# The first four hidden tiles of each down projection are loaded into the raw weight ring

## The chip, the cores and the metric

The kernel runs on one core of one Trainium2 chip. The metric is the device time of one execution in microseconds; a profiled execution has a span (first to last instruction) and a time of its own that is a little longer. Both are given below.

## The reference, cut to what matters

Two layers, each a mixer (stick-breaking attention with an S5 scan in the first, gated delta rule in the second) followed by a squared-ReLU MLP. The change lies in the MLP, which runs once in each layer:

```python
def sq_relu_mlp(h, w1, w2):            # h: 1040 x 1024, w1: 1024 x 4096, w2: 4096 x 1024
    return jnp.square(jax.nn.relu(h @ w1)) @ w2
...
    hn = rms_norm(hs, pre_mlp_norm[i])
    hs = hs + rms_norm(sq_relu_mlp(hn, mlp_w1[i], mlp_w2[i]), post_mlp_norm[i])
return hs[:, N_META:]
```

There are 1024 tokens and 16 meta tokens in front of them, so 1040 columns (NT); the model width is 1024 and the hidden width 4096. All of it is float32.

## The kernel before, in words

**Layout and precision.** Activations lie transposed: the feature is the partition, the token the column. Every float32 factor of a matmul is split into a high part (a cast to the matmul's float32r format) and a low part (the value minus the high part), and each product is three matmuls: high by high, low by high, high by low (`unit`, L176 to L178). For weights the two parts are `whi` and `wlo`, for the hidden activations of the down projection `hh` and `hl`.

**Buffers.** All large tiles come out of one ring of 33 slots of 128 by 1048 (`slot`, tag `r4`): the split activations, the accumulators `acc`, the hidden tiles. Beside them stand two raw tiles of 128 by 1040 (`raw`, tag `wraw`), into which every weight tile is loaded before it is split, and four `whi` and four `wlo` tiles. A matmul accumulates in one of eight PSUM banks: three named `mm`, three `tr`, two `ax`.

**The MLP (`mlp`), up phase.** The hidden activations are computed 128 rows at a time and written to DRAM (`hd`, 32 tiles): six tiles directly (`up`), the other 26 in 13 pairs (`pair`), each a Strassen-like product of seven half-size products (`product`, L478 to L480). `ops` loads the two weight tiles of a pair into the two raw tiles and forms seven operands from them. The result of a product goes through VectorE (L487, and L491 for the ReLU), ScalarE squares it (L415) and a DMA writes it out (L416); its temporaries are called p, u and c.

**The MLP, down phase.** `acc`, eight accumulators, then 14 groups of two hidden tiles and a last group of four (`down`). For group g the code asks for `hidden(2g)` and `hidden(2g+1)`, then for the two w2 tiles (`weight`, with `act=True`):

- `hidden(k)` loads row tile k of `hd` into a raw buffer named `hr` (L529, on SyncE's DMA queue), ScalarE casts it to `hh` (L228), GpSimd subtracts to `hl` (L229).
- `weight` loads a w2 tile into one of the two `wraw` tiles (L156, the same DMA queue), ScalarE casts `whi` (L163), GpSimd subtracts `wlo` (L166).
- `gemm` then walks eight output tiles m and, in each, the column chunks (three of 352, 344, 344 columns in the first layer; two of 512 in the second). One such (m, chunk) is a unit: six matmuls for the group's two k, then VectorE copies the PSUM bank to `acc` (L552, first group) or adds it to `acc` (L554, later groups). A group has 24 units in the first layer and 16 in the second. Six PSUM banks are used in turn (`six`).

Below, h0, h1, ... stand for the hidden tiles in this phase and w0, w1, ... for the w2 tiles; group 0 is h0, h1 with w0, w1, group 1 is h2, h3 with w2, w3.

**What sets the order.** The code's order is not the order on the engines. The framework schedules each engine's instructions when the program is built, and it hands out the buffers of a ring while it does so. What it settles is fixed: each engine, and SyncE's DMA queue too, then works its list strictly in order and stops at an instruction whose buffer or input is not there. One list on SyncE issues nearly all transfers of the kernel; the casts of hidden and weight tiles and the squares of the up phase share ScalarE's list, and the subtractions share GpSimd's.

Of the kernel before, what the change touches and what calls it, by code (L numbers as in the profile page):

```python
# [50 lines left out]
class Net:  # L51
# [349 lines left out]
    def mlp(self, layer, st, hs_d, chunks, gpre, ahead=None):  # L401
# [122 lines left out]

        def hidden(k):

            raw = self.slot("hr")
            hi, lo = self.slot("hh", F32R), self.slot("hl", F32R)
            nc.sync.dma_start(raw[:, t0:NT], hd[:, k, t0:NT])  # L529
            self.split(hi[:, t0:NT], lo[:, t0:NT], raw[:, t0:NT], lo_eng=nc.gpsimd)  # L530
            hid[k] = (hi, lo)

        def down(ks, last=False):
            first = ks[0] == 0
            for k in ks:
                hidden(k)
            W = {k: self.weight(w2[layer, k], act=True) for k in ks}
            out, hook, ch = None, None, wide
            if last:
                ch = chunks  # L540
                if ahead is None:
                    ch = CH3
                if ahead is not None:
                    ahead()
                ssq = self.slot("ssq_o")
                reuse = [t for k in ks for t in hid[k]]
                *out, hook = self.residual(acc, ssq, reuse, G_POSTMLP + 8 * layer, hs_d, gpre, ch)

            def ev(m, c, pt):
                o, n = ch[c]  # L550
                if first:
                    nc.vector.tensor_copy(acc[m][:, o:o + n], pt)  # L552
                else:
                    nc.vector.tensor_add(acc[m][:, o:o + n], pt, acc[m][:, o:o + n])  # L554
                if last:
                    self.sq_acc(ssq, m, m == 0, acc[m][:, o:o + n], o, n)

            self.gemm(range(8), ks, lambda m, k: tuple(w[:, m * 128:(m + 1) * 128] for w in W[k]), lambda k: hid[k], ch, "c" if last else "m", ev, hook, None if last else six)
            for k in ks:
                del hid[k]  # L560
            return out
# [1583 lines left out]
```

## Time and profile before

| | |
|---|---|
| Time, 3 executions | 2953.96, 2966.62, 2972.64 us; median 2966.62 |
| Profiled execution: its time | 2961.22 us |
| Profiled execution: its span | 2959.2 us |
| Mean granted TensorE clock | 0.942 |
| TensorE matmul busy | 2771.1 us, 94% of the span |
| TensorE weight load busy | 2506.0 us, 85% |
| VectorE, ScalarE, GpSimd busy | 1764.7, 1064.4, 1311.6 us |
| Transfers | 360.99 MB, mean 122 GB/s |

In the rows of the profile, a group of instructions reads: line, engine, operation, output tile <- input tiles, shapes, count, and behind a bar its busy time, the mean of one in ns, and the idle time of the engine just before, with what ended it. A row of the timeline reads: start in us, duration, engine, line, operation, tiles, count, and in brackets the idle time before it and its releaser. PE is TensorE, PEld its weight loads, DVE VectorE, ACT ScalarE, POOL GpSimd, SPq SyncE's DMA queue. A row that merges n instructions (xn) gives the start of the first and the time until the last has ended. In the row of a stretch, behind the busy times of the five engines, stand the granted clock, the DMA share and GB/s. The first layer's MLP passes from the up phase to the down phase at about 1047 to 1069 us of the span, the second layer's at about 2554 to 2575 us.

### The profile page before, as it was taken

To read this page: it belongs to the slowest core of one execution; us is meant where nothing else is said; L and a number is where in the kernel's file an instruction comes from. 1 tells how busy PE (TensorE), PEld (TensorE's weight loads), DVE (VectorE), ACT (ScalarE), POOL (GpSimd) and SP (SyncE) were. 2 spreads that over 40 slices of the span, in tenths; PEclk is the share of its full clock that TensorE was granted. 3 is DMA by queue.
4 is the path that set the end of the run, shared out by engine and by line. 5 is a ranking of instruction groups with operands and counts; after the bars stand their busy time and mean duration, and the time that the engine had idled before them with its cause. 6 is when DMAs were issued, how large, how long until landed. Compare 5 with 4: busy or idle time off the path is not lost. (4 is left out here: it accounts for less than half of the span.)

```text
span 2959.2 us, 44165 instructions
## 1 busy us (share of the span) xinstructions
PE 2771.1 (94%) x16488; PEld 2506.0 (85%) x16488; DVE 1764.7 (60%) x3107; ACT 1064.4 (36%) x2108; POOL 1311.6 (44%) x942
## 2 busy tenths in 40 slices
PE   7799998999999999999897978999998999999997
PEld 6689666888999999999887877889998888878887
DVE  8643778677665555555846995444537444544445
ACT  4111556554543332110436322444435433321201
POOL 5561325225577755342522132111135777655423
PEclk9899568899999999999998988999999999999999
DMA  3435212134433343221426667443424333333222
GB/s 128 155 129 161 78 46 88 47 100 167 133 114 102 105 150 130 87 85 57 132 92 216 204 207 208 144 131 126 141 90 158 111 114 107 128 142 100 94 83 87
DMA packets 209766, 360.99 MB, mean 122 GB/s; under 512 B 45488, under 2 KB 131200, under 8 KB 209552
## 3 DMA queue, kind: packets, MB, share of 16 engines
q1 hardware_dynamic: 205664, 353.49, 37.0%
q10 hardware_dynamic: 3888, 4.69, 0.4%
q8 instruction: 130, 2.13, 0.3%
q14 instruction: 84, 0.69, 0.1%
HBM read 247.07 MB, written 111.03 MB: 121 GB/s over the span
## 5 line engine op out<-in xcount | busy, mean ns | idle before, releaser
L166 POOL TENSOR_TENSOR wlo<-wraw,whi 128x1024 fp32r<-128x1024 f32 x129 | 316.4, 2466 | 786.0 <-ACT whi L163 303.4
L176 PE MATMUL mm<-ahi,whi 128*128 128x344 f32 (+2 forms) x1200 | 416.1, 347 | 43.0 <-DVE cx L1333 29.2
L178 PE MATMUL mm<-ahi,wlo 128*128 128x344 f32 (+2 forms) x1200 | 397.3, 331 | 2.3 <-DVE wlo L166 2.3
L177 PE MATMUL mm<-hl,whi 128*128 128x352 f32 (+4 forms) x1136 | 388.8, 342 | 7.2 <-POOL hl L229 7.2
L554 DVE TENSOR_TENSOR acc<-mm,acc 128x344 f32<-128x344 f32 (+4 forms) x308 | 177.3, 576 | 198.2 <-PE mm L178 198.2
L176 PEld LDWEIGHTS mm<-ahi,whi 128*128 128x128 f32 x1200 | 233.8, 195 | 51.2 <-DVE cx L1333 30.7
L176 PE MATMUL mm<-hh,whi 128*128 128x352 f32 (+4 forms) x752 | 260.0, 346 | 5.3 <-ACT hh L228 4.6
L178 PE MATMUL mm<-hh,wlo 128*128 128x352 f32 (+4 forms) x752 | 259.9, 346 | 5.0 <-POOL wlo L166 5.0
L178 PEld LDWEIGHTS mm<-ahi,wlo 128*128 128x128 f32 x1200 | 233.2, 194 | 4.4 <-DVE wlo L166 3.2
L177 PEld LDWEIGHTS mm<-hl,whi 128*128 128x128 f32 x1136 | 218.1, 192 | 19.6 <-POOL hl L229 8.4
L554 DVE TENSOR_TENSOR acc<-tr,acc 128x344 f32<-128x344 f32 (+2 forms) x260 | 152.9, 588 | 137.2 <-PE tr L178 137.2
L163 ACT CAST whi<-wraw 128x1024 fp32r<-128x1024 f32 x77 | 77.5, 1044 | 361.1 <-PE tr L177 357.9
L177 PE MATMUL tr<-hl,whi 128*128 128x512 f32 (+2 forms) x560 | 197.2, 352 | 0.0
L178 PE MATMUL tr<-hh,wlo 128*128 128x512 f32 (+2 forms) x560 | 197.1, 352 | 0.0
L176 PE MATMUL tr<-hh,whi 128*128 128x512 f32 (+2 forms) x560 | 196.9, 352 | 0.0
L229 POOL TENSOR_TENSOR hl<-hr,hh 128x1040 fp32r<-128x1040 f32 (+1 forms) x64 | 155.2, 2434 | 84.6 <-ACT hh L228 69.3
L178 PEld LDWEIGHTS mm<-hh,wlo 128*128 128x128 f32 x752 | 142.8, 190 | 16.6 <-POOL wlo L166 6.2
L176 PEld LDWEIGHTS mm<-hh,whi 128*128 128x128 f32 x752 | 142.7, 190 | 16.3 <-ACT hh L228 5.3
L440 POOL TENSOR_TENSOR wlo<-sS,whi 128x512 fp32r<-128x512 f32 x104 | 144.6, 1393 | 13.8 <-ACT whi L439 13.7
L228 ACT CAST hh<-hr 128x1040 fp32r<-128x1040 f32 (+1 forms) x64 | 67.4, 1054 | 172.3 <-DMA hr<-hd 164.2
L177 PE MATMUL mm<-hh,whi 128*128 128x344 f32 (+2 forms) x384 | 129.3, 337 | 0.0
L244 POOL TENSOR_TENSOR ssq<-ssq,sq 128x344 f32<-128x344 f32 (+2 forms) x84 | 91.4, 1088 | 84.6 <-ACT sq L243 76.6
(526 smaller groups left out, 7825.8 us busy)
## 6 DMA issues: line engine op xcount, KB each, us to landing
wraw<-w SPq DMA_DIRECT2D x128, 512.0 KB, 3.6
hr<-hd SPq DMA_DIRECT2D x32, 520.0 KB, 5.4
wraw<-wino SPq DMA_DIRECT2D x32, 512.0 KB, 5.0
hr<-hd SPq DMA_DIRECT2D x32, 512.0 KB, 4.4
dm<-dmd SPq DMA_DIRECT2D x16, 520.0 KB, 5.5
hsd<-hs SPq DMA_DIRECT2D x48, 172.0 KB, 1.9
hd<-u SPq DMA_DIRECT2D x52, 130.0 KB, 3.3
hd<-u SPq DMA_DIRECT2D x26, 256.0 KB, 2.2
```

Source lines behind the costliest of these rows:

```text
L163: nc.scalar.copy(hi[:, :n], raw[:, :n])
L166: (nc.vector if fast else nc.gpsimd).tensor_sub(lo[:, :n], raw[:, :n], f(hi[:, :n]))
L176: nc.tensor.matmul(pt, wh, h[:, o:o + n], start=i == 0, stop=False)
L177: nc.tensor.matmul(pt, wh, l[:, o:o + n], start=False, stop=False)
L178: nc.tensor.matmul(pt, wl, h[:, o:o + n], start=False, stop=i == len(kts) - 1)
L228: nc.scalar.copy(hi, src)
L229: (lo_eng or nc.vector).tensor_sub(lo, src, f(hi))
L244: nc.gpsimd.tensor_add(st["ssq"][:, o:o + n], st["ssq"][:, o:o + n], sq[:, :n])
L440: nc.gpsimd.tensor_sub(lo, src, f(hi))
L554: nc.vector.tensor_add(acc[m][:, o:o + n], pt, acc[m][:, o:o + n])
```

## The change

One line of `hidden` in `mlp`. For k below 4 the raw data of a hidden tile goes into a tile of the two-buffer ring `wraw`, the ring of the raw weights, and no longer into a slot of `r4`. This holds in both layers, so for eight of the 64 hidden tiles. The split tiles `hh` and `hl`, the transfers' bytes and the arithmetic are the same.

```diff
         def hidden(k):
 
-            raw = self.slot("hr")
+            raw = self.raw() if k < 4 else self.slot("hr")
             hi, lo = self.slot("hh", F32R), self.slot("hl", F32R)
             nc.sync.dma_start(raw[:, t0:NT], hd[:, k, t0:NT])
             self.split(hi[:, t0:NT], lo[:, t0:NT], raw[:, t0:NT], lo_eng=nc.gpsimd)
```

Since buffers come free at other times, the scheduler also orders the lists anew at the passage into the down phase of each layer; elsewhere the lists are as they were. The places below are those of the first layer. In them `p_`, `c_` and `u_` with a number are the temporaries of the last pair of the up phase.

ScalarE's list, from behind the first two copies of the last pair to the first casts of group 2. Before:

```order
L228 CAST hh<-hr 128x1040
L163 CAST whi<-wraw 128x1024
L415 ACTIVATE p_10824<-p_10824 128x260
L228 CAST hh<-hr 128x1040
L415 ACTIVATE p_10839<-p_10839 128x260
L163 CAST whi<-wraw 128x1024
L415 ACTIVATE c_10948<-c_10948 128x260
L415 ACTIVATE c_10966<-c_10966 128x260
L163 CAST whi<-wraw 128x1024
L415 ACTIVATE u_10918<-u_10918 128x260
L415 ACTIVATE u_10933<-u_10933 128x260
L415 ACTIVATE u_10854<-u_10854 128x260
```

```order
L163 CAST whi<-wraw 128x1024
L415 ACTIVATE u_10869<-u_10869 128x260
L163 CAST whi<-wraw 128x1024 x2
L228 CAST hh<-hr 128x1040 x6
L163 CAST whi<-wraw 128x1024 x2
```

The second piece follows directly on the first. Now, from the last square of the last pair on:

```order
L415 ACTIVATE u_10854<-u_10854 128x260
L415 ACTIVATE u_10869<-u_10869 128x260
L228 CAST hh<-wraw 128x1040 x2
L163 CAST whi<-wraw 128x1024 x2
L228 CAST hh<-hr 128x1040
L163 CAST whi<-wraw 128x1024 x2
L228 CAST hh<-hr 128x1040 x4
```

Before, all six weight tiles w0 to w5 were cast ahead of h2; now h2 and h3 are cast ahead of w2 and w3, and h4 ahead of w4 and w5. The casts of h0 and h1 moved up as well, to either side of the copy of p_10839.

SyncE's DMA queue, from the last transfer of the pair before the last on. Before:

```order
L416 DMA hd<-u_10605 128x260
L529 DMA hr<-hd 128x1040 x2
L156 DMA wraw<-w 128x1024
L416 DMA hd<-p_10824 128x260
L416 DMA hd<-p_10839 128x260
L156 DMA wraw<-w 128x1024
L416 DMA hd<-c_10948 128x260
```

```order
L416 DMA hd<-u_10869 128x260
L156 DMA wraw<-w 128x1024
L529 DMA hr<-hd 128x1040
L156 DMA wraw<-w 128x1024
L529 DMA hr<-hd 128x1040
L156 DMA wraw<-w 128x1024
L529 DMA hr<-hd 128x1040 x5
```

And now:

```order
L416 DMA hd<-u_10605 128x260
L156 DMA wraw<-w 128x1024 x2
L416 DMA hd<-p_10824 128x260
L529 DMA wraw<-hd 128x1040
L416 DMA hd<-p_10839 128x260
L529 DMA wraw<-hd 128x1040
L416 DMA hd<-c_10948 128x260
```

```order
L416 DMA hd<-u_10869 128x260
L156 DMA wraw<-w 128x1024 x2
L529 DMA hr<-hd 128x1040
L156 DMA wraw<-w 128x1024 x2
L529 DMA hr<-hd 128x1040
L156 DMA wraw<-w 128x1024 x2
L529 DMA hr<-hd 128x1040 x4
```

Before, w0 and w1 were loaded ahead of the first piece, h0 and h1 at its second row; its two weight loads are w2 and w3, those of the second piece w5, w6 and w7 (w4 lies between the pieces), so h2 stands behind w5 and h3 behind w6. Now h0 and h1 are loaded where w0 and w1 were, w0 and w1 at the second row of the first piece, h2 and h3 between the writes of p and c, and w2 and w3 behind the last write of the up phase. On GpSimd the order is hl, wlo, hl, five wlo, six hl before, and hl, hl, wlo, wlo, hl, hl, wlo, wlo, hl, wlo, wlo now. TensorE's list differs only in the first units of group 1.

## The prediction

> **What bounds the kernel now.** I read the page first. TensorE is busy for nearly the whole span, so only time in which it stands still or runs slowly can be won, and the change touches only the two passages into a down phase. There I read the waits of TensorE in the stretches 1040 to 1150 us (first layer) and 2550 to 2650 us (second), one pair of rows each:
>
> ```profile
> PE 2771.1 (94%) x16488; PEld 2506.0 (85%) x16488; DVE 1764.7 (60%) x3107; ACT 1064.4 (36%) x2108; POOL 1311.6 (44%) x942
> ...
> PE mm L177 <- POOL hl L229: 3.5, 1, 3.5
> PE mm L176 <- ACT hh L228: 2.5, 1, 2.5
> ...
> PE mm L177 <- POOL hl L229: 3.7, 1, 3.7
> PE mm L176 <- ACT hh L228: 2.2, 1, 2.2
> ```
>
> In each layer TensorE waits twice, for the cast `hh` and then for the difference `hl` of a hidden tile: 6.0 us idle in the first layer, 5.9 us in the second. The idle time is not the whole loss. In the rows by stretch the seventh value behind the stretch is the granted clock:
>
> ```profile
> 1088.00:1092.00 4.00, 1.54 (x8) 1.26 (x7) 0.52 (x1) 2.70 (x3) 3.13 (x2) 0.91 0.00 0
> 1092.00:1096.00 4.00, 0.53 (x3) 0.09 (x2) 0.00 (x0) 0.09 (x1) 3.87 (x2) 0.50 0.94 345
> 1096.00:1100.00 4.00, 4.00 (x14) 4.00 (x15) 0.00 (x0) 1.15 (x2) 2.41 (x1) 0.50 0.97 315
> ...
> 2600.00:2604.00 4.00, 1.01 (x2) 0.83 (x3) 0.00 (x0) 0.00 (x0) 2.93 (x2) 0.50 0.78 286
> 2604.00:2608.00 4.00, 4.00 (x13) 3.18 (x12) 0.00 (x0) 2.10 (x2) 1.35 (x1) 0.65 1.02 414
> ```
>
> Once TensorE has stood, it is granted half its clock, and keeps it for some time after work is back (0.50 from 1092 to 1100 with TensorE fully busy in its second half). The whole loss I therefore measure by output: VectorE copies one PSUM bank for each unit, and the copies have an even beat. Timeline of VectorE, the 17th and the 24th (last) unit of group 0 and the 7th of group 1, for each layer:
>
> ```profile
> 1081.70 0.52 DVE L552 COPY acc<-mm 128x344 f32<-128x344 f32 x1 [0.41 <-PE mm L178]
> 1088.34 0.52 DVE L552 COPY acc<-tr 128x344 f32<-128x344 f32 x1 [0.43 <-PE tr L178]
> 1104.47 0.52 DVE L554 TENSOR_TENSOR acc<-mm,acc 128x352 f32<-128x352 f32 x1
> ...
> 2586.00 0.69 DVE L552 COPY acc<-mm 128x512 f32<-128x512 f32 x1 [0.69 <-PE mm L178]
> 2595.71 0.69 DVE L552 COPY acc<-tr 128x512 f32<-128x512 f32 x1 [0.69 <-PE tr L178]
> 2613.85 0.69 DVE L554 TENSOR_TENSOR acc<-mm,acc 128x512 f32<-128x512 f32 x1 [0.29 <-PE mm L178]
> ```
>
> (In the second layer these are the 9th and 16th of group 0.) Seven units take 1088.34 - 1081.70 = 6.64 us undisturbed; between the last of group 0 and the seventh of group 1 pass 16.13 us. So 9.49 us are lost. In the second layer: 18.14 - 9.71 = 8.43 us. I take the seventh because the first six wait in PSUM, half done, until the stall ends. Together **17.92 us**, 0.61% of the span.
>
> **Why h2 and h3 are late** is in ScalarE's and SyncE's lists, both in order (first layer):
>
> ```profile
> 1069.56 0.42 ACT L415 ACTIVATE u<-u 128x260 f32<-128x260 f32 x1
> 1087.75 1.99 ACT L163 CAST whi<-wraw 128x1024 fp32r<-128x1024 f32 x2 [17.77 <-PE tr L177]
> 1089.65 1.05 ACT L228 CAST hh<-hr 128x1040 fp32r<-128x1040 f32 x1
> 1095.91 1.06 ACT L228 CAST hh<-hr 128x1040 fp32r<-128x1040 f32 x1 [5.21 <-DMA hr<-hd]
> ...
> 1072.65 0.37 SPq L529 DMA_DIRECT2D hr<-hd  x1
> 1091.69 0.37 SPq L529 DMA_DIRECT2D hr<-hd  x1
> ```
>
> h2 is on its way at 1072.65, but its cast stands behind the casts of w4 and w5. These need `whi` tiles that group 0 still reads, so ScalarE sits idle for 17.77 us, until group 0 is done. h3's load stands behind w6's on SyncE, which needs the raw tile of w4, so it goes out only at 1091.69. Neither tile lacks a slot; both are queued behind something for group 2 or 3. The stall is one of order.
>
> **The change, part by part.** It removes no instruction and no byte. It moves the casts and differences of h2 and h3 ahead of w2 to w5, and puts the weights behind the hidden tiles in the ring of two raw tiles: h0, h1, then w0, w1, then h2, h3, then w2, w3. Each step of this ring waits until the step before has been split. I replay the chain with these rows (means in ns; of the transfers the median to landing, and for `hr` also the spread):
>
> ```profile
> L166 POOL TENSOR_TENSOR wlo<-wraw,whi 128x1024 fp32r<-128x1024 f32 x129 | 316.4, 2466 | 786.0 <-ACT whi L163 303.4
> L163 ACT CAST whi<-wraw 128x1024 fp32r<-128x1024 f32 x77 | 77.5, 1044 | 361.1 <-PE tr L177 357.9
> L229 POOL TENSOR_TENSOR hl<-hr,hh 128x1040 fp32r<-128x1040 f32 (+1 forms) x64 | 155.2, 2434 | 84.6 <-ACT hh L228 69.3
> L228 ACT CAST hh<-hr 128x1040 fp32r<-128x1040 f32 (+1 forms) x64 | 67.4, 1054 | 172.3 <-DMA hr<-hd 164.2
> wraw<-w SPq DMA_DIRECT2D x128, 512.0 KB, 3.6
> DMA to landing us min/median/max: 3.4/4.5/9.0
> ```
>
> So hh 1.05, hl 2.43, a weight's landing 3.6, whi 1.04, wlo 2.47 us.
>
> *Group 0 (new cost, if any).* Its operands can begin when the raw tiles and the first slots are free, and must be there when its first unit is computed. What the trace has of both, first layer, then second:
>
> ```profile
> 1036.46 0.33 SPq L156 DMA_DIRECT2D wraw<-w  x1
> 1041.78 0.33 SPq L156 DMA_DIRECT2D wraw<-w  x1
> 1047.49 0.89 SPq L529 DMA_DIRECT2D hr<-hd  x2
> ...
> 1048.33 0.38 ACT L496 COPY p<-tr 128x260 f32<-128x260 f32 x1
> ...
> 1060.34 2.60 POOL L166 TENSOR_TENSOR wlo<-wraw,whi 128x1024 fp32r<-128x1024 f32 x1
> ...
> 1068.98 0.52 DVE L552 COPY acc<-mm 128x352 f32<-128x352 f32 x1
> ...
> 2554.53 1.28 POOL L440 TENSOR_TENSOR wlo<-sS,whi 128x512 fp32r<-128x512 f32 x1 [2.59 <-ACT whi L439]
> 2567.57 2.40 POOL L166 TENSOR_TENSOR wlo<-wraw,whi 128x1024 fp32r<-128x1024 f32 x1
> ...
> 2565.37 0.64 ACT L415 ACTIVATE p<-p 128x512 f32<-128x512 f32 x1 [2.40 <-DVE p L491]
> 2575.61 0.64 ACT L415 ACTIVATE u<-u 128x512 f32<-128x512 f32 x1 [1.08 <-DVE u L491]
> ...
> 2575.50 0.68 DVE L552 COPY acc<-mm 128x512 f32<-128x512 f32 x1
> ```
>
> The raw tiles were free at 1036.46 and 1041.78, where w0 and w1 were loaded; h0 and h1 now take these places and are landed long before a slot is free. That is at 1047.49, where `hr` was issued. The cast of h0 goes ahead of the copy at 1048.33, so hh0 ends near 1049.4, hl0 at 1051.8, hl1 at 1054.3; w1 lands at 1057.9, whi1 ends at 1058.9, or about 1 us later behind a square of p, and wlo1 at 1062.4. Before, wlo1 ended at 1062.94: the long preload of w0 and w1 was worth nothing, because `wlo` waited its turn on GpSimd. The first copy of group 0 comes at 1068.98, so the slack is some 6.5 us. Second layer: GpSimd is free at 2555.81, hl1 ends at 2560.7, w1 lands at 2564.3, whi1 stands behind the square that ends at 2566.01 and ends at 2567.05, wlo1 at 2569.5, against 2569.97 before and a first copy at 2575.50: slack 6.0 us. With the longest landing of `hr`, 9.0 us, both chains are 5.4 us later and still just in time. Cost zero.
>
> The copy of p_10839 comes about 1.4 us later on ScalarE, since hh0 stands in front of it. Its cover is the ring of seven PSUM banks of the up phase; with one bank held 1.4 us longer, six others are left, and each takes one product of 12 matmuls. I take zero, at most 1.4 us in the first layer alone.
>
> *Group 1 (the gain).* h2 and h3 are cast after the last square, at 1069.98: hh2 to 1071.0, hl2 to 1073.5, hl3 to 1075.9. w2 is loaded behind hl2, lands at 1077.1, whi2 to 1078.1, wlo2 to 1080.6; w3 behind hl3, 1079.5, 1080.5, and wlo3, after wlo2, to **1083.0**. Group 0 ends at 1088.34: slack 5.3 us. Second layer: last square to 2576.25, hl3 to 2582.2, w3 landed 2585.8, wlo3 to **2589.3**, against 2595.71: slack 6.4 us. The stall goes whole: -9.49 and -8.43 us. With a landing of 9.0 us wlo3 ends at 1088.4 and 2594.7, so at worst about 1 us of the first comes back.
>
> *Group 2 (where the wait could go next).* h4 is split before the casts of w4 and w5, h5 behind them. These still wait for the end of group 0: whi5 to 1089.7 as now, two wlo to 1093.9, hl5 to 1096.3. Group 2 begins 24 beats of 0.949 us after 1088.34, at 1111.1. Nothing is late next, and from there the lists repeat as before, four GpSimd operations of some 2.45 us in each 22.8 us.
>
> **Sum**: 0 - 9.49 - 8.43 + 0 = -17.9 us; bounds -15.5 (1.4 and 1 us come back) and -17.9, as the beat cannot be better than undisturbed. The profiled execution's 2961.22 us would become 2943.3. It was 5.4 us faster than the median of the three runs, 2966.62, from which I forecast **2948.7 us**.
>
> [...]
>
> **The rivals.**
>
> *Part of it comes back.* The weights of group 1 are now last in the ring, with four steps that wait on each other. If each landing takes 9 us and the squares end a few us later, wlo3 is 2 to 5 us late in each layer; the gain is 9 to 13 us, the time about 2956. For it: four of its steps also queue on GpSimd. Against it: 5.3 and 6.4 us of slack, of which the longest landing alone takes 5.4.
>
> *It does not do what the order says*: TensorE stalls as before, now for w2 and w3. That needs wlo3 about 9 us behind group 0's end, 14 us behind my replay; 2966.6. No row shows a step that long.
>
> *Slower: group 0 starts late.* The mechanism is the ring at the start: w0 and w1 are loaded only after hl0 and hl1. Should these wait for the end of the last pair (about 1068 us), because the slots of hh or hl are given late, TensorE would stand for 1.05 + 2.43 + 2.43 + 3.6 + 1.04 + 2.47 = 13.0 us in each layer and about 3 us more at half clock. That is +32.0 - 17.9 = +14.1, so 2980.7 us. It decides once group 0 starts 6 us late: then twice 6 us and 3 us of slow clock have eaten the 17.9. Against it: `hr` found its slot at 1047.49, 20 us before.
>
> **How the numbers follow.** The forecast (at least 14 us won) gets 0.80, part of it 0.10, no gain 0.05, slower 0.05. The three runs of before lie 12.7 us below to 6.0 us above their median, so the forecast itself reaches from 2936 to 2955; the range must take in the partial case at 2956 and some spread above, and I give 2936 to 2962. What can be told from no change is about 1% of this kernel, 30 us. The whole loss at both places is 17.9 us, so faster by over 1% needs the spread of the runs as well: 0.05. Slower by over 1% is the last rival with the same spread: 0.03. Within 1%: 0.92.
>
> **What would show it.** Right: in the waits of TensorE in both passages the two rows above are gone; the clock stays at 1.00 through the end of group 0; from group 0 to group 1 VectorE's beat of 0.95 and 1.39 us goes on; ScalarE casts two `hh` right after the last square, and `wlo` of w3 ends near 1083 and, the second layer being 9.5 us earlier by then, near 2580. Group 0's first copy still comes without a wait. Wrong: a wait of TensorE for `wlo` or `whi` at the start of group 0 or 1, a new one for `hl` at group 2, or a loss of beat before 1069 us.

## The result, and the profile after

The change made the kernel faster by 0.7%: 2947.59 us (median of 6 runs, 2943.85 to 2951.62) against 2969.95 us (6 runs, 2953.96 to 2979.15), a ratio of 0.993 with a 95% interval of 0.9912 to 0.9949. That is a gain of about 15 to 26 us; the forecast was 2948.7 us and a gain of 17.9. The profiled execution took 2945.58 us with a span of 2943.5 us, at a mean granted clock of 0.944 (before: 2961.22, 2959.2, 0.942).

In this execution the first layer's passage lies some 5.7 us later than in that of before, because earlier parts of it, where nothing was changed, took longer. Times of the two are therefore compared only as differences.

Waits of TensorE from 1040 to 1150 us; those from 2540 to 2650 us look the same:

```profile
core 0 of [0], span 2943.5 us
engine line waited for: us in total, times, longest us
```

The list is empty. Before, two rows stood here in each layer. The stretches at the end of group 0 and the start of group 1, first layer, then second:

```profile
1092.00:1096.00 4.00, 4.00 (x28) 4.00 (x27) 2.03 (x5) 2.50 (x3) 1.37 (x1) 1.00 0.00 0
1096.00:1100.00 4.00, 4.00 (x27) 4.00 (x26) 2.27 (x6) 0.46 (x1) 4.00 (x3) 1.00 0.39 131
...
2586.00:2590.00 4.00, 4.00 (x19) 3.27 (x18) 2.00 (x3) 2.67 (x3) 3.14 (x2) 1.00 0.00 0
2590.00:2594.00 4.00, 4.00 (x19) 3.26 (x18) 1.91 (x4) 0.00 (x0) 4.00 (x2) 1.00 0.66 218
```

TensorE is busy for all of each stretch, and the clock stays at 1.00 where it had stood at 0.50. The same copies of VectorE as before: the 17th and 24th of group 0 and the 7th of group 1, and for the second layer the last of group 0 and the 7th of group 1:

```profile
1087.43 0.52 DVE L552 COPY acc<-mm 128x344 f32<-128x344 f32 x1 [0.42 <-PE mm L178]
...
1094.08 0.52 DVE L552 COPY acc<-tr 128x344 f32<-128x344 f32 x1 [0.42 <-PE tr L178]
...
1100.77 0.53 DVE L554 TENSOR_TENSOR acc<-mm,acc 128x352 f32<-128x352 f32 x1 [0.45 <-PE mm L178]
...
2586.61 0.69 DVE L552 COPY acc<-tr 128x512 f32<-128x512 f32 x1 [0.69 <-PE tr L178]
...
2596.32 0.69 DVE L554 TENSOR_TENSOR acc<-mm,acc 128x512 f32<-128x512 f32 x1 [0.69 <-PE mm L178]
```

1100.77 - 1094.08 = 6.69 us, less the undisturbed 6.64: 0.05 us lost, where it had been 9.49. In the second layer 9.71 - 9.71 = 0.00, where it had been 8.43. Below, "the loss" of a layer is always this difference.

ScalarE (first layer) and then GpSimd show the order that did it:

```profile
1072.15 0.42 ACT L415 ACTIVATE u<-u 128x260 f32<-128x260 f32 x1 [1.01 <-DVE u L491]
1072.48 2.00 ACT L228 CAST hh<-wraw 128x1040 fp32r<-128x1040 f32 x2
1079.33 1.05 ACT L163 CAST whi<-wraw 128x1024 fp32r<-128x1024 f32 x1 [4.84 <-DMA wraw<-w]
1082.31 1.05 ACT L163 CAST whi<-wraw 128x1024 fp32r<-128x1024 f32 x1 [1.93 <-DMA wraw<-w]
```

```profile
1062.27 4.95 POOL L166 TENSOR_TENSOR wlo<-wraw,whi 128x1024 fp32r<-128x1024 f32 x2 [2.31 <-ACT p L415]
1073.60 4.83 POOL L229 TENSOR_TENSOR hl<-wraw,hh 128x1040 fp32r<-128x1040 f32 x2 [6.39 <-ACT hh L228]
1080.51 2.41 POOL L166 TENSOR_TENSOR wlo<-wraw,whi 128x1024 fp32r<-128x1024 f32 x1 [2.08 <-ACT whi L163]
1083.49 2.41 POOL L166 TENSOR_TENSOR wlo<-wraw,whi 128x1024 fp32r<-128x1024 f32 x1 [0.57 <-ACT whi L163]
```

The two `hh` follow the last square at once. `wlo` of w3, the last piece of group 1, is ready at 1083.49 + 2.41 = 1085.90, which is 8.2 us before the last copy of group 0; in the second layer it is ready at 2579.62, 7.0 us before.

The two spans differ by 15.7 us. From the `whi` cast of the last pair (L439) to the 7th copy of group 1, the passage took 58.87 us before and 49.50 now, in the second layer 60.02 and 51.47: together 17.9 us less. In the rest of the program, which the change leaves alone, this execution was 2.2 us slower.

### The profile page after: what moved, and what is told of

It is laid out like the page before. It is cut to its first block, busy times and chain, and to the rows that moved or that the text cites. A ratio compares the mean times of both kernels' runs of the same rounds, so it can differ in the third digit from the quotient of the medians.

```text
span 2943.5 us, 44168 instructions
## 1 busy us (share of the span) xinstructions
PE 2767.2 (94%) x16488; PEld 2505.5 (85%) x16488; DVE 1752.0 (60%) x3107; ACT 1063.4 (36%) x2108; POOL 1305.4 (44%) x942
## 5 line engine op out<-in xcount | busy, mean ns | idle before, releaser
L178 PE MATMUL mm<-ahi,wlo 128*128 128x344 f32 (+2 forms) x1200 | 400.3, 334 | 2.3 <-DVE wlo L166 2.3
L178 PE MATMUL mm<-hh,wlo 128*128 128x352 f32 (+4 forms) x752 | 260.4, 347 | 5.0 <-POOL wlo L166 5.0
L178 PEld LDWEIGHTS mm<-ahi,wlo 128*128 128x128 f32 x1200 | 235.5, 196 | 4.3 <-DVE wlo L166 3.2
L178 PE MATMUL tr<-hh,wlo 128*128 128x512 f32 (+2 forms) x560 | 196.1, 350 | 0.0
L229 POOL TENSOR_TENSOR hl<-hr,hh 128x1040 fp32r<-128x1040 f32 (+1 forms) x56 | 135.6, 2429 | 78.0 <-ACT hh L228 62.3
L178 PEld LDWEIGHTS mm<-hh,wlo 128*128 128x128 f32 x752 | 143.1, 191 | 16.5 <-POOL wlo L166 6.2
L366 POOL TENSOR_TENSOR ssq_o<-ssq_o,sq 128x344 f32<-128x344 f32 (+4 forms) x84 | 93.9, 1117 | 79.8 <-ACT sq L365 79.3
```

The lines of the kernel that those rows point to most:

```text
L178: nc.tensor.matmul(pt, wl, h[:, o:o + n], start=False, stop=i == len(kts) - 1)
L229: (lo_eng or nc.vector).tensor_sub(lo, src, f(hi))
L366: nc.gpsimd.tensor_add(ssq[:, o:o + n], ssq[:, o:o + n], sq[:, :n])
```

## The experiments

Two theories stood against each other. **Order** (the prediction's): h2 and h3 were late only because their cast and load stood in ScalarE's and SyncE's lists behind the casts of w4, w5 and the load of w6. **Slots**: the eight tiles that leave the ring `r4` free its slots, and that is what lets work start earlier. The losses of all kernels, in us:

| kernel | loss, 1st layer | loss, 2nd layer | time, us | ratio, 95% interval |
|---|---|---|---|---|
| before | 9.49 | 8.43 | 2965.26, 2965.50, 2965.76 beside the three batches | |
| the change | 0.05 | 0.00 | 2947.59 | 0.993 (0.9912 to 0.9949) |
| e_h01 | 9.35 | 8.67 | 2965.02 | 1.0001 (0.9988 to 1.0014) |
| e_h23 | 0.06 | 0.00 | 2945.49 | 0.9924 (0.9905 to 0.9944) |
| e_order | 0.01 | 0.00 | 2944.05 | 0.9919 (0.9905 to 0.9934) |
| e_l0 | 0.05 | 8.90 | 2954.41, once | |
| e_sub2 | 0.05 | 0.01 | 2949.90, once | |
| e_sub3 | 0.26 | 1.48 | 2957.52, once | |
| e_sub4 | 8.20 | 7.17 | 2953.82, once | |
| e_all | 0.05 | 0.04 | 2948.03 | 0.9946 (0.993 to 0.9963) |
| e_h2 | 1.90 | 0.06 | 2961.80, once | |
| e_h3 | 6.94 | 6.07 | 2964.16, once | |
| chg_again | 0.05 | 0.01 | 2948.93 | 0.994 (0.9921 to 0.9958) |
| order_again | 0.01 | 0.00 | 2947.90 | 0.9935 (0.9919 to 0.9951) |

Times of one execution say little: six runs of chg_again reach from 2941.24 to 2959.44, and in the one run of e_h2 the last pair came 15 us later than in that of the change (its L439 cast at 1066.54 us, against 1051.27), in parts that no edit touches. Where a kernel ran once, the losses decide.

**Only h0 and h1 in the raw ring.**

```diff
-            raw = self.raw() if k < 4 else self.slot("hr")
+            raw = self.raw() if k < 2 else self.slot("hr")
```

> Only h0 and h1 go into the raw ring, h2 and h3 into slots again. The lists then put six weight casts ahead of h2, as before the change. I measure each layer by the time from the last copy of group 0 to the seventh copy of group 1, less seven undisturbed beats (6.64 and 9.71 us): 9.49 and 8.43 us lost before, 0 expected after. Theory (what counts is that h2 and h3 stand ahead of w4 and w5): nothing is won, 8 to 10 us lost in each layer, waits of TensorE for hh and hl as before, time as before the change (within 4 us). Rival one (slots: two raw tiles fewer in the slots let the later ones go sooner): half the gain, 9 us. Rival two (the gain comes from the earlier start of h0 and h1): all of it, 18 us.

Nothing is gained. Waits of TensorE in the first layer, and ScalarE's list there:

```profile
PE mm L177 <- POOL hl L229: 3.2, 1, 3.2
PE mm L176 <- ACT hh L228: 2.5, 1, 2.5
```

```profile
1089.04 1.99 ACT L163 CAST whi<-wraw 128x1024 fp32r<-128x1024 f32 x2 [19.76 <-PE tr L177]
1090.94 1.05 ACT L228 CAST hh<-hr 128x1040 fp32r<-128x1040 f32 x1
```

The casts of w4 and w5 still stand in front of h2's, and ScalarE still waits in front of them, now for 19.76 us. Half of the freed slots does nothing for the stall.

**Only h2 and h3.**

```diff
-            raw = self.raw() if k < 4 else self.slot("hr")
+            raw = self.raw() if k in (2, 3) else self.slot("hr")
```

> Only h2 and h3 go into the raw ring, h0 and h1 into slots as before. The lists put h2 and h3 ahead of w2 and w3, as in the change. Theory (order): the whole gain, both losses below 0.5 us, no wait of TensorE in either passage, time as with the change, 18 us below before. Rival one (slots): half, 9 us. Rival two (start of h0 and h1): nothing, as before.

All of the gain, with no wait of TensorE at either passage. With e_h01 this puts the effect on h2 and h3 alone, but both theories can still claim it.

**No raw ring at all, another order in the code.** The tiles stay in `r4` as before; `down` asks for all four hidden tiles ahead of the first weight.

```diff
-            raw = self.raw() if k < 4 else self.slot("hr")
+            raw = self.slot("hr")
...
-            for k in ks:
-                hidden(k)
+            for k in range(4) if first else ks:
+                k in hid or hidden(k)
```

> All hidden tiles stay in slots as before; only the code asks for h2 and h3 ahead of w0 and w1, and the lists put their casts between the casts of w1, w2 and w3. Theory (order alone): both losses below 0.5 us, 18 us won, without any use of the raw ring. Rival (the slots that the raw ring saves): nothing won, time as before. If h2 and h3 in slots delay w0 and w1 on GpSimd (two more differences of 2.43 us ahead of w2 and w3), it shows at group 1, not at group 0, since their order against w0 and w1 is kept.

This decides against the slots: with the slots of before, the loss is gone. ScalarE in the first layer:

```profile
1070.88 1.06 ACT L228 CAST hh<-hr 128x1040 fp32r<-128x1040 f32 x1 [3.37 <-DMA hr<-hd]
...
1074.66 1.06 ACT L228 CAST hh<-hr 128x1040 fp32r<-128x1040 f32 x1 [0.83 <-DMA hr<-hd]
...
1094.66 2.00 ACT L163 CAST whi<-wraw 128x1024 fp32r<-128x1024 f32 x2 [16.84 <-PE tr L177]
```

h2 and h3 are cast before the last square. The casts of w4 and w5 still wait, for 16.84 us, and it costs nothing, since nothing near stands behind them. It has a small price of its own in the first layer, which the loss, counted from the last copy of group 0, does not show: VectorE's first copy of group 0 comes 4.4 us later behind the L439 cast than with the change (25.33 against 20.93 us), TensorE waits once for 0.3 us for it (`acc`, L552), and group 0 ends 0.5 us later (43.29 against 42.81 us; 43.32 in order_again).

**The change in the first layer alone.**

```diff
-            raw = self.raw() if k < 4 else self.slot("hr")
+            raw = self.raw() if k < 4 and layer == 0 else self.slot("hr")
```

> The change in the first layer alone. Theory: the loss of the first layer is gone (9.49 to 0), that of the second is as before (8.43), so the passage terms add up: time between before and the change, some 9 us below before. Rival (the layers influence each other, or the gain is spread over later groups): a loss in the first layer, or one well below 8 us in the second.

0.05 us are lost in the first layer and 8.90 in the second, where both waits are back (2.9 for `hl`, 2.2 for `hh`). The two passages add up; neither hides the other.

**How much slack the new chain has.** The difference `hl` of h2 and h3 is formed twice, three times, four times, with the same result, so GpSimd's part of the chain grows by some 4.9 us a step.

```diff
-            hid[k] = (hi, lo)
+            hid[k] = (hi, lo); [nc.gpsimd.tensor_sub(lo[:, t0:NT], raw[:, t0:NT], f(hi[:, t0:NT])) for _ in range(1) if k in (2, 3)]
```

(`range(2)` and `range(3)` for three and four times. The repetitions stand in L531 of the profile.)

> The change, with the differences hl of h2 and h3 done twice each on GpSimd (same result), which holds the ring's steps back by 2 x 2.43 = 4.9 us in each layer. With the change wlo of w3 ended 8.2 us (first layer) and 7.0 us (second) before the last copy of group 0. Theory (slack): wlo of w3 ends 4.9 us later, 3.3 and 2.1 us before that copy, nothing lost. Rival (the ring is on the edge): a loss of some 5 us in each layer.

> As the run before, three times each: 9.7 us later. [...]

> Four times each: 14.6 us later. Theory: wlo of w3 ends 6.3 and 7.5 us behind the last copy of group 0; TensorE waits about 6 and 7 us, the clock falls to 0.5 and the loss is 8 to 10 and 10 to 11 us, as much as before the change. Rival (slow clock costs nothing beside the wait): loss equal to the wait.

One repetition is free. With two, `wlo` of w3 is ready 1.3 and 2.5 us behind the last copy of group 0, and 0.26 and 1.48 us are lost: less than the lateness, because TensorE has the other products of the first units to do. With three, the stall is back, now for `wlo`. GpSimd, first layer:

```profile
1081.75 2.44 POOL L229 TENSOR_TENSOR hl<-hr,hh 128x1040 fp32r<-128x1040 f32 x1
1084.14 2.43 POOL L531 TENSOR_TENSOR hl<-wraw,hh 128x1040 fp32r<-128x1040 f32 x1
1086.51 2.35 POOL L166 TENSOR_TENSOR wlo<-wraw,whi 128x1024 fp32r<-128x1024 f32 x1
1088.80 2.42 POOL L229 TENSOR_TENSOR hl<-hr,hh 128x1040 fp32r<-128x1040 f32 x1
1091.17 4.74 POOL L166 TENSOR_TENSOR wlo<-wraw,whi 128x1024 fp32r<-128x1024 f32 x2
```

`wlo` of w3 (the first of the pair at 1091.17) ends some 8.2 us behind the last copy (1085.35), in the second layer 9.4 us. The added work alone would make it 6.3 and 7.5 us (six operations of some 2.42 us, less the slack of 8.2 and 7.0). The rest comes from order again: the scheduler put the difference of h4 (`hl<-hr`, at 1081.75) ahead of the last one of h3 (at 1084.14), so h3's raw tile came free for w3 one operation later, and w3's `whi` waited for its load until 1089.84. (The difference of h5, at 1088.80, also stands ahead, but `whi` of w3 was ready only at 1090.89.) This wait has its own price in clock:

```profile
1084.00:1088.00 4.00, 1.79 (x12) 1.50 (x10) 1.03 (x2) 1.04 (x1) 4.00 (x3) 1.00 0.11 24
1088.00:1092.00 4.00, 3.09 (x11) 3.00 (x12) 0.00 (x0) 1.05 (x1) 4.00 (x3) 0.52 0.81 296
1092.00:1096.00 4.00, 3.44 (x12) 3.00 (x12) 1.37 (x3) 2.10 (x2) 4.00 (x3) 0.50 0.54 198
1096.00:1100.00 4.00, 4.00 (x21) 4.00 (x20) 1.56 (x3) 1.05 (x1) 4.00 (x2) 0.70 0.73 273
```

TensorE waits for 3.7 us (two waits, the longer 3.1), and 8.20 us are lost; in the second layer it waits for 5.3 us and loses 7.17. The expectation had waits of 6 and 7 us, and 10 to 11 us lost in the second layer.

**Every hidden tile in the raw ring.**

```diff
-            raw = self.raw() if k < 4 else self.slot("hr")
+            raw = self.raw()
```

> All 32 hidden tiles of each down phase go through the two raw tiles. Theory (slack of the ring): from the end of group g-2, two weight splits (about 7 us), a load of two hidden tiles (to 8 us), two casts and differences (to 14 us), two weight loads (to 17 us) fit into a group of 22.8 and 22.2 us, so no new wait: time as with the change, within 5 us. Rival (two raw tiles bound the down phase once every tile goes through them): a wait in nearly each of the 28 groups, more than 50 us slower than with the change.

Nothing lost, nothing more won: the ring of two carries all 64 hidden tiles and all weights, TensorE waits for nothing from 1040 to 1150 and from 2540 to 2650 us, as in the changed kernel, and the time is 2948.03 us against its 2947.59. Had freed slots been worth time, 56 more tiles out of `r4` should have shown it.

**h2 alone, h3 alone.**

```diff
-            raw = self.raw() if k < 4 else self.slot("hr")
+            raw = self.raw() if k == 2 else self.slot("hr")
```

> Only h2 goes into the raw ring. In the lists h2's cast now stands behind w3's and ahead of w4's, h3's cast still behind w4's. Theory (each tile costs what its own place in the lists makes it late): with E the end of group 0, whi of w4 ends at E + 0.5, hh of h3 at E + 1.5, wlo of w4 at E + 2.9 and hl of h3 at E + 5.3. Meanwhile TensorE has all of k = 2 for six units (18 matmuls, 2.9 us in the first layer, 4.1 in the second) and the first products of k = 3 (1.0 and 1.4 us). So the wait for hh is gone and that for hl falls to some 1.5 us in the first layer and none in the second; loss 1 to 3 and 0 to 1 us, clock at 1.00. Rival (the stall is one thing and stays until both tiles are moved): 8 to 9 us in each layer.

```diff
-            raw = self.raw() if k < 4 else self.slot("hr")
+            raw = self.raw() if k == 3 else self.slot("hr")
```

> Only h3 goes into the raw ring. h2's cast stands behind w4's, h3's behind h2's. Theory: hh of h2 at E + 1.5, wlo of w4 at E + 2.9, hl of h2 at E + 5.3, hl of h3 at E + 7.7. TensorE waits for hh (1.5 to 2 us) and again for hl (2.5 to 3 us), the clock falls in the second wait, and the loss is 6 to 8 us in each layer: most of the stall stays. Rival (h3's late load on SyncE, which this removes, was the larger part): a loss below 4 us.

With h2 alone, ScalarE in the first layer has:

```profile
1096.48 1.06 ACT L228 CAST hh<-wraw 128x1040 fp32r<-128x1040 f32 x1
1108.68 1.05 ACT L163 CAST whi<-wraw 128x1024 fp32r<-128x1024 f32 x1 [11.14 <-PE tr L177]
1109.63 1.06 ACT L228 CAST hh<-hr 128x1040 fp32r<-128x1040 f32 x1
```

h2 is cast in time and only h3 stands behind w4. TensorE waits once, for 1.6 us, and 1.90 us are lost; in the second layer nothing, where TensorE had enough to do in longer units (1.387 us) to cover nearly the same delay: `hl` of h3 ended 5.3 us behind the last copy in the first layer, 5.0 us in the second. With h3 alone, h2 stands behind w4, though h3 has its place in the ring:

```profile
1097.40 1.05 ACT L163 CAST whi<-wraw 128x1024 fp32r<-128x1024 f32 x1 [12.15 <-PE tr L177]
1098.35 1.05 ACT L228 CAST hh<-hr 128x1040 fp32r<-128x1040 f32 x1
1099.31 1.06 ACT L228 CAST hh<-wraw 128x1040 fp32r<-128x1040 f32 x1
```

6.94 and 6.07 us are lost. So the right place for h2 alone wins 16.0 of the 17.9 us (17.92 - 1.96), that for h3 alone 4.9 us (17.92 - 13.01): the tile that is needed first carries most of it.

**The change and the other order, again.** Both kernels once more, on one chip, to compare their times.

> The change itself once more, on the same chip as the next kernel, to compare the two. Theory: 0.993 of before, 18 us below.

> The kernel that only asks for h2 and h3 earlier and keeps all hidden tiles in slots, once more. Theory (both remove the same stall and nothing else): the same time as the change within 3 us. Rival (one of them has a further effect): a difference of more than 3 us that holds over the rounds.

2948.93 us (2941.24 to 2959.44) and 2947.90 us (2941.17 to 2949.63): not to be told apart. No kernel here beats the change by what can be measured.

## Why the prediction was right

**The loss of before (17.92 us), read by the beat.** Right, and so was its size: the two passages became 17.9 us shorter. By the idle time alone the forecast would have been 11.9 us, outside the measured gain of 15 to 26. That the forecast time lies within 1.1 us of the measured median is partly luck: between the medians the gain is 22.4 us here and 16.8 us in chg_again, and what bears the forecast out is the passages.

**The cause, order and not slots.** Shown from both sides: the order without the raw ring takes the whole loss away (e_order), the freed slots of h0 and h1 without the order take none (e_h01), and 56 more of them add none (e_all).

**Group 0 costs nothing.** Right. `wlo` of w1 was replayed to 1062.4, or 1068.1 on the new time axis; it ended at 1062.27 + 4.95 = 1067.22. VectorE's first copy:

```profile
1071.69 0.43 DVE L491 SCALAR_TENSOR_TENSOR u<-u,rb 128x260 f32<-128x260 f32 x1
1072.20 0.53 DVE L552 COPY acc<-mm 128x352 f32<-128x352 f32 x1
```

The copy starts 5.0 us behind that, instead of the 6.5 predicted, and 6.4 instead of 6.0 in the second layer (2559.47 to 2565.89). But the first copy was the wrong mark for the slack: it waits for VectorE's L491, while TensorE needs `wlo` of w1 earlier. This is the first matmul that reads it (the second L178 of group 0), before and then after the change:

```profile
1066.17 0.32 PE L178 MATMUL mm<-hh,wlo 128*128 128x352 f32 x1
...
1071.84 0.32 PE L178 MATMUL mm<-hh,wlo 128*128 128x352 f32 x1
```

Both stand 20.57 us behind the L439 cast, so TensorE lost nothing here. The replayed slack was 3.8 us and not 6.5, the measured one 4.6; in the second layer 5.0 replayed and 6.0 measured. The prediction's "still just in time" with a landing of 9 us, 5.4 us later, does not hold by this mark. The term of up to 1.4 us for the copy of p_10839 did not appear: from the L439 cast to the last copy of group 0 the first layer took 42.81 us against 42.74 before.

**Group 1.** Right in kind, too careful in size: slack 8.2 us where 5.3 was replayed, and 7.0 where it was 6.4. The replay started from the last square at its old place, but that square came some 3 us earlier relative to the beat in the first layer and 0.6 us in the second. The likely reason is below, in what was not expected. e_sub2 bears the size out: one more pair of differences, 4.9 us, was still free.

**Group 2.** Right: no wait up to 1150 and 2650 us.

**The clock.** The measured loss was the right price of these stalls: the passages gave 17.9 us. Beside the idle time, before paid 9.49 - 6.0 = 3.5 us in the first layer and 8.43 - 5.9 = 2.5 us in the second; the 3 us of slow clock that the prediction's last rival adds in each layer lie at the mean of these two. In the first layer the clock fell once, at 1091.25, 0.5 us after the first wait had ended, and stayed at 0.50 through the second until 1101.49. TensorE worked for 6.8 us of that time. Counted as half speed, an estimate, that costs 3.4 us beside the 5.9 idle: 9.3 of the 9.49. (In the first layer its matmuls follow each other every 0.29 us at 0.50 and every 0.16 at 1.00.) In the second layer it worked for 3.8 us at 0.50, by the same estimate 1.9 + 5.9 = 7.8 of the 8.43.

**The rivals.** A part coming back (2956) needed the chain 2 to 5 us late, and it was early by 7 to 8. No gain, and group 0 late, each had a row against it, and both rows held: no step of the new chain was as long as the first needed, and `hh` of h0 was cast at 1053.99, 17 us before TensorE's first unit.

## What to carry to other kernels

When an engine's list is fixed, an idle time in front of an instruction says nothing yet; look at what stands behind it. Here a prefetch for group 2 held the cast for group 1, and the cure was to put the near work ahead; the buffer was only the means that moved it, and two lines of code order did the same. Price such a stall by the output beat across it, since the slow clock can cost more than the wait itself (4.5 us beside 3.7 in e_sub4's first layer).

## What the runs showed of the hardware that was not expected

**At the passages the clock fell with as little as 1.8 us of idle time behind it, and stayed low for one, two or three steps of 3.41 us.** The granted clock stood at 0.50 for 10.24 us in the first layer of before and of e_sub4, for 6.82 us in the second layer of before and the first of e_h3, for 3.41 us in the second layers of e_sub4 and e_h3: each time a whole number of steps of 3.41 us, as far as the rows tell. The moments follow from the rows by stretch (4 us at a mean of 0.62 hold 3.0 us at half); those of before are read from stretches of 0.05 us. The row that follows the prediction's three of the first layer before:

```profile
1100.00:1104.00 4.00, 4.00 (x23) 4.00 (x22) 2.09 (x5) 3.34 (x4) 3.04 (x2) 0.81 0.97 392
```

The falls at the two passages lie whole steps apart: in before, the clock falls at 1091.25 and again at 2599.94, 442 steps of 3.4133 us later; in e_sub4 (1088.16 and 2590.00) and e_h3 (1100.96 and 2606.24) they lie 440 and 441 such steps apart. Whether what a wait does depends on where it lies against these steps was not shown, since no run moved one wait along them. The wait of 1.6 us in e_h2 left the clock at 1.00 and cost 0.3 us beyond itself (1.90 - 1.6); a wait of 1.1 us in the second layer of e_sub3 left it at 1.00 too. In e_h3's first layer it fell at 1100.96, with 1.8 us of idle time behind it: a wait of 1.5 us and the first 0.3 us of the next, of 2.6. This cost 6.94 us:

```profile
1100.00:1104.00 4.00, 1.38 (x7) 1.10 (x6) 0.00 (x0) 0.37 (x1) 4.00 (x3) 0.62 0.51 179
1104.00:1108.00 4.00, 4.00 (x14) 3.56 (x14) 1.04 (x2) 2.11 (x2) 4.00 (x3) 0.53 0.54 208
1108.00:1112.00 4.00, 4.00 (x28) 4.00 (x27) 2.51 (x5) 0.00 (x0) 2.36 (x1) 1.00 0.77 276
```

In e_sub4's first layer it fell at 1088.16, 2.4 us into the wait of 3.1, and came back at 1098.40. The idle time and, by the estimate above, half of the work done at 0.50 give nearly the whole loss there too: 3.7 + 8.9 / 2 = 8.2 us of 8.20. So the fall came with 1.8 us (e_h3), 2.4 us (e_sub4) and 2.5 us (before) of idle time behind it in the first layers, and the recovery one, two or three steps after the fall.

**VectorE's L491 took up to 2.57 us beside GpSimd's differences, and 0.43 us alone.** The ReLU step L491 reads two SBUF tiles. Before, five of the last eight of the last pair took 1.55 to 2.46 us, each ending some 0.3 us after the GpSimd subtraction beside it; the others took 0.43. VectorE before, then GpSimd before:

```profile
1053.08 2.46 DVE L491 SCALAR_TENSOR_TENSOR p<-p,rb 128x260 f32<-128x260 f32 x1
...
1065.08 2.38 DVE L491 SCALAR_TENSOR_TENSOR u<-u,rb 128x260 f32<-128x260 f32 x1
...
1067.83 0.43 DVE L491 SCALAR_TENSOR_TENSOR u<-u,rb 128x260 f32<-128x260 f32 x1
```

```profile
1052.83 2.43 POOL L229 TENSOR_TENSOR hl<-hr,hh 128x1040 fp32r<-128x1040 f32 x1 [5.24 <-ACT hh L228]
...
1064.76 2.42 POOL L166 TENSOR_TENSOR wlo<-wraw,whi 128x1024 fp32r<-128x1024 f32 x1 [1.81 <-ACT whi L163]
```

The one that starts at 1053.08 ends at 1055.54, just behind the 1055.26 of the subtraction, while L487 at 1055.46, which reads a PSUM bank and one SBUF tile, takes 0.41 us beside the next subtraction. In the changed kernel only one of the eight took longer, 1.56 us. The last square and group 0's first copy came about 2.4 to 3 us earlier against the beat, which this would explain and which is the slack that the replay lacked; no run tried it by itself. In e_order, where two more subtractions fall beside the last two of the eight, those took 2.57 and 2.19 us, up to 2.1 more than the 0.43 alone, and its first copy came 4.4 us later, as told above. The end of group 0 did not move, as the 42.81 us above show.

**Hidden tiles land sooner from the alternating ring.** In e_all the 64 loads of hidden tiles land within these times, where before they took 3.4, 4.5 and 9.0:

```profile
DMA to landing us min/median/max: 3.2/3.3/5.0
```

Why was not tried. The time did not change.
